# Seven-product matmul phases of a decoder trunk: sums of the moving operand on another engine, a second place for shared sums, stores two steps later, differences spread

## The chip, the cores and the metric

The kernel runs on one core of a Trainium2 chip. The metric is the device time in microseconds (us). Three runs of the kernel before gave 1637.1 (median), 1635.87 and 1639.43.

## What is computed

One layer of a hybrid decoder trunk over 1056 tokens: 1024 of a prompt and 32 new ones (8 sequences of 4). A normalised input goes through one wide projection; sliding-window attention and a gated linear recurrence run side by side, their outputs are mixed by sigmoid gates, and an MLP and a per-layer embedding follow. The last part of the reference is the part that the change touches:

```python
rnn = (h.astype(x.dtype) * jax.nn.gelu(gr)) @ lw['w_o_rnn']
mix = (jax.nn.sigmoid(ga_logit) * (att @ lw['w_o_attn']) + jax.nn.sigmoid(gr_logit) * rnn) @ lw['w_out']
x = x + mix
hmid = jax.nn.relu(rmsnorm(x, lw['norm2_g']) @ lw['w_up'])
x = x + (hmid * hmid) @ lw['w_down']
gate = jax.nn.sigmoid(rmsnorm(x, lw['ple_norm_g']) @ lw['w_ple_gate'])
x = x + gate * (p.astype(x.dtype) @ lw['w_ple'])
```

`D_MODEL` is 1024 and `D_FF` 4096. All data is float32.

## The kernel before

**Phases.** The matmuls from `w_o_rnn` to `w_down` run as ten phases of equal size (list `phases`): `rnn` (w_o_rnn), `out` (w_out), and then four times `up` and `down`, each on a quarter of the MLP's inner width. Each phase multiplies a 1024x1024 weight by a 1024x1056 moving operand. It cuts both into 2x2 blocks and computes seven products of blocks instead of eight, which needs sums of blocks on both sides and sums of the results (`PRODUCTS`: which weight sum meets which operand sum, q = 0 to 6). Blocks of the weight are called A11 to A22 and their sums S1 to S4; blocks of the operand B11 to B22 and their sums T1 to T4.

**Steps.** A product is four steps (p = 0 to 3, one for each 128 output rows); a step is 24 matmuls of 128x264, since each float32 operand is split into a high and a low part and three of the four part products are computed (lines 1432 to 1434). So a phase has 28 steps, and all phases 280. The main loop over `s` writes out the order of each engine by hand, step by step: `prepare` (the weights' high part by ScalarE, `w_high`, L1131, and low part by VectorE, `w_low`, L1136), `down_sums` (sums of weight blocks, by accumulating DMAs on GpSimd's queue, in every phase but the three later `up`), the step's matmuls, `evacuate` of the step before, the `hooks` of this step, and `prepare_b`. `flow.later(n, f)` runs f at the end of the n-th step from now, this one counted as the first. Each engine, and each DMA queue, works in the order in which its instructions were written out; a wait holds up all that stands behind it on the same engine or queue.

**The moving operand.** `prepare_b` does two things for the products to come. `b_sums` makes the operand's sums in place: for q = 2 with VectorE (L1150, L1151); for q = 3 and 4, in the phases rnn, out and the first up, with ScalarE (a negation, L1153) and accumulating DMAs from GpSimd's queue (L1154, L1156); in the phase down with VectorE, for q = 4 and 5 (L1158, L1160). `b_split` then splits a block into high (ScalarE, L1174) and low part (VectorE, L1175) in one of four places of `ring`; two places belong to one product, and a place is written again two products, eight steps, later. The half k2 = 0 of a product's sums is written out at the last step of the product two before it, its split at the first step of the product before it; the half k2 = 1 follows at the first and second step of the product before it. In the first up phase the split parts also go to DRAM (`xc_dram`, L1178, on the sync engine's queue), and the three later up phases read them from there (L1169) instead of splitting again.

**Evacuation.** `evacuate` adds a step's result to the quarters of the output to which it belongs (`put`, VectorE, L1227), or copies it where the quarter is empty (ScalarE, L1233). In phase out the quarters are the residual X, and products 1 to 3 are also gathered in a tile `shared`, one for each p (L1254 and L1227), which GpSimd's queue adds to other rows of X by accumulating DMAs (L1259): once after product 2, twice after product 3. Rows that are complete are squared and summed (`squares`, L1197, L1198) and scaled for the next phase (`scaled_row`, L1364). `mean_square` multiplies the sums of squares by a matrix of ones (L1352). In phase rnn, `mix` multiplies by a gate (L1336) and adds the attention part, twelve times of sixteen by an accumulating DMA (L1340).

**Hooks.** `hook(s, f)` puts f at step s. `differences(p)` (L1280), two subtractions on VectorE on rows of X that phase down adds to, stands at steps 84 to 87, the first four of the first down phase.

Of the kernel before, what the change touches and what calls it, by code (L numbers as in the profile page):

```python
# [13 lines left out]
F32 = mybir.dt.float32  # L14
F32R = mybir.dt.float32r
AF = mybir.ActivationFunctionType
ALU = mybir.AluOpType

P = 128
# [8 lines left out]
TH, CQ = T // 2, T // 4  # L28
# [62 lines left out]
def trunk(ctx: ExitStack, tc: tile.TileContext, I, O):  # L91
    nc = tc.nc
    PE, ACT, DVE, POOL, SP = nc.tensor, nc.scalar, nc.vector, nc.gpsimd, nc.sync

    def f32(ap):
        return ap.bitcast(F32)

    ctx.enter_context(tc.manual_schedule())
    flow = Flow()
# [856 lines left out]
    HALF = [slice(0, TH), slice(TH, T)]  # L956
# [95 lines left out]
    xc_dram = spill.tile([28, P, 2, TH], F32, name="xc_dram")  # L1052
    X, xn, shared = [None] * KT, [[None, None] for _ in range(4)], {}
# [14 lines left out]
    def b_view(ph_, k2, kh_, th_):  # L1068

        kind, f = phases[ph_]  # L1070
        if kind == "rnn":
            return [rnn[4 * kh_ + 2 * k2 + i][:, HALF[th_]] for i in range(2)]
        return [(xn if kind == "up" else hid)[k2 + 2 * kh_][th_]]
# [3 lines left out]
    def later_up(ph_):  # L1077
        kind, f = phases[ph_]
        return kind == "up" and f > 0
# [58 lines left out]
    def of_product(g):  # L1138
        return g // 7, g % 7

    def b_sums(g, k2):

        ph_, q = of_product(g)
        kind, f = phases[ph_]
        if kind == "up" and f:
            return
        by_dma = kind != "down"
        for b11, b12, b21, b22 in zip(*(b_view(ph_, k2, kh_, th_) for kh_, th_ in ((0, 0), (0, 1), (1, 0), (1, 1)))):
            if q == 2:
                DVE.tensor_tensor(b12, b22, b12, op=ALU.subtract)  # L1150
                DVE.tensor_tensor(b11, b12, b11, op=ALU.add)  # L1151
            elif q == 3 and by_dma:
                ACT.activation(b11, b11, AF.Identity, scale=-1.0)  # L1153
                POOL.dma_start(b21, b11, accum_op=ALU.add)  # L1154
            elif q == 4 and by_dma:
                POOL.dma_start(b11, b22, accum_op=ALU.add)  # L1156
            elif q == 4:
                DVE.tensor_tensor(b21, b21, b11, op=ALU.subtract)  # L1158
            elif q == 5 and not by_dma:
                DVE.tensor_tensor(b11, b22, b11, op=ALU.subtract)  # L1160

    def b_split(g, k2):
        ph_, q = of_product(g)
        kind, f = phases[ph_]
        r = ring[2 * (g % 2) + k2]
        u = 4 * q + 2 * k2
        if kind == "up" and f:
            for k in range(2):
                SP.dma_start(f32(r[:, k]), xc_dram[u + k])  # L1169
            return  # L1170
        src = b_view(ph_, k2, *B_HOME[PRODUCTS[q][1]])
        for i, x in enumerate(src):
            hi, lo = (r[:, :, n, :] if len(src) == 1 else r[:, i, n, :] for n in range(2))
            ACT.copy(hi, x)  # L1174
            DVE.tensor_tensor(lo, x, f32(hi), op=ALU.subtract)  # L1175
        if kind == "up":
            for k in range(2):
                SP.dma_start(xc_dram[u + k], f32(r[:, k]))  # L1178

    x2 = {}  # L1180

# [11 lines left out]
    def squares(j, th_, eng):  # L1193
        x, o = X[j][:, HALF[th_]], HALF[th_]
        if th_ in summed:
            s = chunk_tmp("t")
            ACT.activation(s, x, AF.Square)  # L1197
            eng.tensor_tensor(ssq2[:, o], ssq2[:, o], s, op=ALU.add)  # L1198
        else:
            ACT.activation(ssq2[:, o], x, AF.Square)  # L1200
            summed.add(th_)
# [11 lines left out]
    def third_gain(j, th_):  # L1213
        third_high(j, th_)
        third_low(j, th_)

    def evacuate(u, ps):
        ph_, q, p = u // 28, u % 28 // 4, u % 4
        kind, f = phases[ph_]

        def quarter(m, th_):
            r = p + 4 * m
            t = hid[r // 2][th_][:, r % 2] if kind in ("up", "rnn") else X[r][:, HALF[th_]]
            return t.rearrange("p (c n) -> p c n", c=2)

        q11, q12, q21, q22 = (quarter(m, th_) for m in range(2) for th_ in range(2))
        put = lambda to, of, op: DVE.tensor_tensor(to, of, ps, op=op)  # L1227
        if kind in ("rnn", "up"):

            sign = 1.0 if later_up(ph_) else -1.0  # L1230
            add, neg = ALU.add, ALU.add if later_up(ph_) else ALU.subtract
            if q < 2:
                ACT.activation((q11, q12)[q], ps, AF.Identity, scale=sign)  # L1233
            for to, of, op in ([], [(q11, q11, neg)], [(q12, q12, add)], [(q22, q12, neg)], [(q21, q22, add)],
                               [(q22, q22, add), (q12, q12, add)], [(q12, q12, neg)])[q]:
                put(to, of, op)
            if q not in (1, 4, 5, 6):
                return
            th_ = int(q > 4)
            if kind == "rnn":  # L1240
                mix(p + 4 * (q in (4, 5)), th_)
                return
            h, r = (q12, q11, q21, q22)[(6, 1, 4, 5).index(q)], ssq[:, HALF[th_]].rearrange("p (c n) -> p c n", c=2)

            def squared_relu():
                DVE.scalar_tensor_tensor(h, h, 0.0, r, op0=ALU.max, op1=ALU.mult)  # L1246
                ACT.activation(h, h, AF.Square, scale=0.5)  # L1247
            flow.later(1, squared_relu)
            return
        if kind == "out":  # L1250

            if q == 1:
                shared[p] = big.tile([P, TH], F32, tag=f"d{4 + p}", name="shared")
                ACT.activation(shared[p].rearrange("p (c n) -> p c n", c=2), ps, AF.Identity, scale=-1.0)  # L1254
            sh = shared[p].rearrange("p (c n) -> p c n", c=2) if q else None
            for to, op in ([(q11, 0)], [(q11, 0)], [(sh, 1)], [(sh, 0)], [(q21, 1)], [(q22, 1), (q12, 1)], [(q12, 0)])[q]:
                put(to, to, (ALU.subtract, ALU.add)[op])
            for r, th_ in {2: ((p, 1),), 3: ((p + 4, 0), (p + 4, 1))}.get(q, ()):
                POOL.dma_start(X[r][:, HALF[th_]], shared[p], accum_op=ALU.add)  # L1259
            if q in (1, 4, 5, 6):  # L1260
                j, th_ = p + 4 * (q in (4, 5)), int(q > 4)
                flow.later(1, lambda: (squares(j, th_, DVE), scaled_row(j, th_)))
            return

        last = ph_ == NPH - 1
        for to, op in ([(q11, ALU.subtract)], [(q11, ALU.subtract), (q22, ALU.subtract)], [(q22, ALU.add)],
                       [(q22, ALU.subtract), (q12, ALU.add)], [(q21, ALU.add)],
                       [(q22, ALU.add)] + ([] if last else [(q21, ALU.subtract)]), [(q12, ALU.subtract)])[q]:
            put(to, to, op)
        if last:  # L1270
            if q == 1:
                flow.later(8, lambda: third_gain(p, 0))
            elif q == 4:
                DVE.tensor_tensor(q21, q21, q22, op=ALU.add)
                flow.later(5, lambda: third_gain(p + 4, 0))
# [50 lines left out]
    def load_sigma(j, th_, place):  # L1326
        sigma_of[j, th_] = place
        SP.dma_start(place, s_dram[j, :, HALF[th_]])
# [4 lines left out]
    def mix(j, th_):  # L1333
        th_ = int(th_)
        u, a = hid[j // 2][th_][:, j % 2], A[j][:, HALF[th_]]
        DVE.tensor_tensor(u, u, sigma_of[j, th_], op=ALU.mult)  # L1336
        if j < 4 and th_ == 1:
            DVE.tensor_tensor(u, u, a, op=ALU.add)
        else:
            POOL.dma_start(u, a, accum_op=ALU.add)  # L1340
# [30 lines left out]
    def hook(s, fn, *args):  # L1371
        hooks.setdefault(s, []).append(lambda: fn(*args))


    for j in range(4):
        hook(2 + j, sigmoid, j, 0)
        hook(10 + j, load_sigma, j + 4, 0, rnn[j][:, HALF[1]])
        hook(12 + j, lambda j=j: load_sigma(j + 4, 1, sigmas[j]))
        hook(14 + j, sigmoid, j + 4, 0)
        hook(15 + j, load_sigma, j, 1, rnn[j + 4][:, HALF[0]])  # L1380
        hook(18 + j, sigmoid, j + 4, 1)
        hook(21 + j, load_residual, j)
        hook(22 + j, sigmoid, j, 1)
        hook(26 + j, load_residual, j + 4)
        hook(84 + j, differences, j)
    hook(28 + 23, second_norm, 0)
    hook(28 + 30, summed.clear)
    hook(56 + 2, second_norm, 1)
# [30 lines left out]
    for s in range(STEPS):  # L1419
        ph_, q, p = s // 28, s % 28 // 4, s % 4  # L1420
# [7 lines left out]
        for c in range(2):  # L1428
            ps = a[:, c, :CQ]
            for k in range(4):  # L1430
                r = ring[2 * (s // 4 % 2) + k // 2][:, k % 2, :, c * CQ:(c + 1) * CQ]
# [79 lines left out]
    for th_ in range(2):  # L1511
        for j in range(KT):
# [8 lines left out]
            for c in range(2):  # L1521
                oc = slice(c * CQ, (c + 1) * CQ)
                ps = a[:, c, :CQ]
# [63 lines left out]
```

## Time and profile before

| | us |
|---|---|
| median of 3 runs | 1637.1 |
| the profiled execution | 1636.45 |
| its span, first to last instruction | 1634.7 |
| phase rnn, from 649.2 | 91.9 |
| phase out, from 741.1 | 100.9 |
| first phase up, from 842.0 | 96.8 |
| first phase down, from 938.8 | 89.7 |
| second phase up, from 1028.5 | 82.1 |
| second phase down, from 1110.6 | 82.2 |

All rows below are of one profiled execution. PE is TensorE, DVE VectorE, ACT ScalarE, POOL GpSimd, SP the sync engine. Times run from the start of the span. A phase is found in the trace by its matmuls: the first 24 of lines 1432 to 1434 are step 0, the next 24 step 1, and so on; it begins where its first matmul begins. PEclk is the clock that TensorE was granted, as a share of 2.4 GHz. The DMA share is the mean busy share of the 16 DMA engines by their packets, and can exceed 1 since packets overlap.

### The profile page before, as it was taken

Reading aid. Unit: us, or ns where it says so; the run is one execution under the profiler, and the core shown is the slowest. Engines: PE = TensorE matmul, PEld = TensorE weight load, DVE = VectorE, ACT = ScalarE, POOL = GpSimd, SP = SyncE. Lnnn points to the kernel's source line nnn. Section 1 sums busy time; section 2 is a strip of 40 time slices with the busy share of each in tenths; the row PEclk is TensorE's granted clock in tenths of the full one; section 3 lists DMA queues with packets and bytes.
Section 4 is the critical chain, followed back from the end, with each engine's and each line's share of the span. In section 5 each row is a group of like instructions: output and inputs, shape, how many; then the busy total and the mean of one; then the engine's idle time right before and its main releaser. Section 6 shows DMA issues by size and latency. Waiting matters only on the chain.

```text
span 1634.7 us, 28211 instructions
## 1 busy us (share of the span) xinstructions
PE 1561.1 (95%) x11488; PEld 1537.9 (94%) x11488; DVE 1072.1 (66%) x1481; ACT 838.7 (51%) x1324; POOL 329.6 (20%) x327
## 2 busy tenths in 40 slices
PE   5989999999999999989989989999999999999997
PEld 5989999999999999989888889999999999999997
DVE  6797665444334353667677698579857985799862
ACT  6555666777667756553484433344334433446341
POOL 4552225232222311322312010001000100012010
PEclk9999999999999999999999999999999999999999
DMA  5522112133321176799979964486348634880332
GB/s 177 81 78 69 54 68 80 59 119 109 109 96 59 46 254 197 162 256 228 209 220 245 307 119 146 177 299 116 134 180 302 115 132 185 298 171 9 97 86 75
DMA packets 186138, 242.08 MB, mean 148 GB/s; under 512 B 22004, under 2 KB 134820, under 8 KB 185992
## 3 DMA queue, kind: packets, MB, share of 16 engines
q1 hardware_dynamic: 150680, 197.93, 36.5%
q0 software_dynamic: 35328, 42.34, 15.7%
q8 instruction: 91, 1.49, 0.4%
q14 instruction: 39, 0.32, 0.1%
HBM read 160.32 MB, written 38.60 MB: 122 GB/s over the span
## 4 chain that ended last, share of the span: by engine, by line
PE 72%; DVE 10%; DMA 8%; ACT 5%; issue 3%; POOL 1%; SPq 1%; ACTq 0%; POOLq 0%; DVEq 0%
PE acc L1433 12%; PE acc L1432 12%; PE acc L1434 12%; PE m L225 9%; PE m L227 9%; PE m L226 9%; DMA gl<-gl 2%; PE acc L1527 2%; PE acc L1529 2%; PE acc L1528 2%; DMA xn<-xn 2%; DMA X<-shared 2%; DVE wul L1136 1%; DVE ring L1175 1%; DMA wblock<-in_w_out 1%
## 5 line engine op out<-in xcount | busy, mean ns | idle before, releaser
L1432 PE MATMUL acc<-ring,wuh 128*128 128x264 f32 x2240 | 641.8, 287 | 24.8 <-DVE hid L1227 12.0
L1433 PE MATMUL acc<-ring,wuh 128*128 128x264 f32 x2240 | 643.6, 287 | 2.5 <-DVE ring L1175 2.5
L1434 PE MATMUL acc<-ring,wul 128*128 128x264 f32 x2240 | 643.9, 287 | 0.0
L1432 PEld LDWEIGHTS acc<-ring,wuh 128*128 128x128 f32 x2240 | 427.2, 191 | 29.1 <-ACT ring L1174 9.5
L1433 PEld LDWEIGHTS acc<-ring,wuh 128*128 128x128 f32 x2240 | 425.5, 190 | 5.0 <-DVE ring L1175 5.0
L1434 PEld LDWEIGHTS acc<-ring,wul 128*128 128x128 f32 x2240 | 425.3, 190 | 0.0
L225 PE MATMUL m<-xa,wh 128*128 128x352 f32 x912 | 298.9, 328 | 0.1
L226 PE MATMUL m<-xb,wh 128*128 128x352 f32 x912 | 295.0, 323 | 1.3 <-DVE xb L319 1.2
L227 PE MATMUL m<-xa,wl 128*128 128x352 f32 x912 | 295.4, 324 | 0.0
L1131 ACT CAST wuh<-wblock 128x1024 fp32r<-128x1024 f32 x100 | 104.5, 1048 | 193.5 <-PE acc L1433 158.1
L226 PEld LDWEIGHTS m<-xb,wh 128*128 128x128 f32 x912 | 173.4, 190 | 2.4 <-DVE xb L319 2.1
L225 PEld LDWEIGHTS m<-xa,wh 128*128 128x128 f32 x912 | 172.9, 190 | 1.1 <-ACT xa L318 0.4
L227 PEld LDWEIGHTS m<-xa,wl 128*128 128x128 f32 x912 | 172.9, 190 | 0.0
L1227 DVE TENSOR_TENSOR X<-X,acc 128x528 f32<-128x528 f32 x180 | 121.1, 697 | 32.4 <-PE acc L1434 28.0
L1227 DVE TENSOR_TENSOR hid<-hid,acc 128x528 f32<-128x528 f32 x140 | 96.2, 700 | 59.5 <-PE acc L1434 37.1
L1136 DVE TENSOR_TENSOR wul<-wblock,wuh 128x1024 fp32r<-128x1024 f32 x100 | 122.0, 1220 | 18.8 <-ACT wuh L1131 18.8
L1096 POOL DMA_DIRECT2D wblock<-wblock x14 | 18.6, 1536 | 492.4 <-DMA wblock<-in_w_down 375.1
L1175 DVE TENSOR_TENSOR ring<-hid,ring 128x1056 fp32r<-128x1056 f32 x70 | 88.8, 1268 | 30.4 <-ACT ring L1174 30.4
L1174 ACT CAST ring<-hid 128x1056 fp32r<-128x1056 f32 x70 | 74.0, 1070 | 59.0 <-DVE hid L1151 15.1
L1247 ACT ACTIVATE hid<-hid 128x528 f32<-128x528 f32 x64 | 41.3, 645 | 92.0 <-DVE hid L1246 92.0
L154 DVE TENSOR_TENSOR wl<-wraw,wh 128x1024 fp32r<-128x1024 f32 (+1 forms) x45 | 54.7, 1216 | 48.7 <-ACT wh L153 48.5
L857 DVE SCALAR_TENSOR_TENSOR rt<-a,rt 128x1056 f32<-128x1056 f32 x8 | 10.1, 1258 | 109.3 <-ACT rt L854 109.3
(348 smaller groups left out, 2525.3 us busy)
## 6 DMA issues: line engine op xcount, KB each, us to landing
ring<-xc_dram SPq DMA_DIRECT2D x84, 528.0 KB
wblock<-in_w_down SPq DMA_DIRECT2D x40, 512.0 KB
wraw<-in_w_in SPq DMA_DIRECT2D x34, 512.0 KB
wblock<-in_w_up SPq DMA_DIRECT2D x34, 512.0 KB
xc_dram<-ring SPq DMA_DIRECT2D x28, 528.0 KB
wblock<-wblock POOLq DMA_DIRECT2D x28, 512.0 KB, 7.4
s<-wblock POOLq DMA_DIRECT2D x28, 512.0 KB, 5.7
wblock<-in_w_o_rnn SPq DMA_DIRECT2D x10, 512.0 KB
```

What stands on the lines that cost most here:

```text
L154: low.tensor_tensor(lo[:, :nk, :], raw[:, :nk, :], f32(hi[:, :nk, :]), op=ALU.subtract)
L225: PE.matmul(ps, wh, xh, start=k == 0, stop=False)
L226: PE.matmul(ps, wh, xl, start=False, stop=False)
L227: PE.matmul(ps, wl, xh, start=False, stop=k == nk - 1)
L1131: ACT.copy(units[u][0], w_view(ph_, PRODUCTS[q][0], p2))
L1136: DVE.tensor_tensor(lo, w_view(ph_, PRODUCTS[q][0], p2), f32(hi), op=ALU.subtract)
L1174: ACT.copy(hi, x)
L1175: DVE.tensor_tensor(lo, x, f32(hi), op=ALU.subtract)
L1227: put = lambda to, of, op: DVE.tensor_tensor(to, of, ps, op=op)
L1432: PE.matmul(ps, wh[:, k, m], r[:, 0, :], start=k == 0, stop=False)
L1433: PE.matmul(ps, wh[:, k, m], r[:, 1, :], start=False, stop=False)
L1434: PE.matmul(ps, wl[:, k, m], r[:, 0, :], start=False, stop=k == 3)
```

## The change

In phases rnn, out and the first up, `b_sums` makes the sums for q = 4 and 5 by VectorE, as in phase down; the negation and the accumulating DMAs of these sums are gone. The tile `shared` has two places: the sum after product 3 is written to the second one, from the first, and each DMA reads the place of its product. The stores of the split parts to `xc_dram` are written out two steps later (by `flow.later`). The four `differences` stand at steps 70, 75, 80 and 85 (56 + 14, 19, 24, 29) instead of 84 to 87; steps 56 to 83 are the first up phase.

```diff
--- before.py
+++ after.py
@@ -1144,19 +1144,13 @@
         kind, f = phases[ph_]
         if kind == "up" and f:
             return
-        by_dma = kind != "down"
         for b11, b12, b21, b22 in zip(*(b_view(ph_, k2, kh_, th_) for kh_, th_ in ((0, 0), (0, 1), (1, 0), (1, 1)))):
             if q == 2:
                 DVE.tensor_tensor(b12, b22, b12, op=ALU.subtract)
                 DVE.tensor_tensor(b11, b12, b11, op=ALU.add)
-            elif q == 3 and by_dma:
-                ACT.activation(b11, b11, AF.Identity, scale=-1.0)
-                POOL.dma_start(b21, b11, accum_op=ALU.add)
-            elif q == 4 and by_dma:
-                POOL.dma_start(b11, b22, accum_op=ALU.add)
             elif q == 4:
                 DVE.tensor_tensor(b21, b21, b11, op=ALU.subtract)
-            elif q == 5 and not by_dma:
+            elif q == 5:
                 DVE.tensor_tensor(b11, b22, b11, op=ALU.subtract)
 
     def b_split(g, k2):
@@ -1174,8 +1168,7 @@
             ACT.copy(hi, x)
             DVE.tensor_tensor(lo, x, f32(hi), op=ALU.subtract)
         if kind == "up":
-            for k in range(2):
-                SP.dma_start(xc_dram[u + k], f32(r[:, k]))
+            flow.later(2, lambda: [SP.dma_start(xc_dram[u + k], f32(r[:, k])) for k in range(2)])
 
     x2 = {}
 
@@ -1250,13 +1243,14 @@
         if kind == "out":
 
             if q == 1:
-                shared[p] = big.tile([P, TH], F32, tag=f"d{4 + p}", name="shared")
-                ACT.activation(shared[p].rearrange("p (c n) -> p c n", c=2), ps, AF.Identity, scale=-1.0)
-            sh = shared[p].rearrange("p (c n) -> p c n", c=2) if q else None
-            for to, op in ([(q11, 0)], [(q11, 0)], [(sh, 1)], [(sh, 0)], [(q21, 1)], [(q22, 1), (q12, 1)], [(q12, 0)])[q]:
-                put(to, to, (ALU.subtract, ALU.add)[op])
+                shared[p] = big.tile([P, 2, TH], F32, tag=f"d{4 + p}", name="shared")
+                ACT.activation(shared[p][:, 0].rearrange("p (c n) -> p c n", c=2), ps, AF.Identity, scale=-1.0)
+            sh, sh2 = (shared[p][:, i].rearrange("p (c n) -> p c n", c=2) for i in range(2)) if q else (None, None)
+            for to, of, op in ([(q11, q11, 0)], [(q11, q11, 0)], [(sh, sh, 1)], [(sh2, sh, 0)], [(q21, q21, 1)],
+                               [(q22, q22, 1), (q12, q12, 1)], [(q12, q12, 0)])[q]:
+                put(to, of, (ALU.subtract, ALU.add)[op])
             for r, th_ in {2: ((p, 1),), 3: ((p + 4, 0), (p + 4, 1))}.get(q, ()):
-                POOL.dma_start(X[r][:, HALF[th_]], shared[p], accum_op=ALU.add)
+                POOL.dma_start(X[r][:, HALF[th_]], shared[p][:, q - 2], accum_op=ALU.add)
             if q in (1, 4, 5, 6):
                 j, th_ = p + 4 * (q in (4, 5)), int(q > 4)
                 flow.later(1, lambda: (squares(j, th_, DVE), scaled_row(j, th_)))
@@ -1382,7 +1376,7 @@
         hook(21 + j, load_residual, j)
         hook(22 + j, sigmoid, j, 1)
         hook(26 + j, load_residual, j + 4)
-        hook(84 + j, differences, j)
+        hook(56 + (14, 19, 24, 29)[j], differences, j)
     hook(28 + 23, second_norm, 0)
     hook(28 + 30, summed.clear)
     hook(56 + 2, second_norm, 1)
```

## Rows read from the trace of the kernel before

**Rows 1.** The page's busy table: busy us (share of the span), instructions.

```profile
PE 1561.1 (95%) x11488; PEld 1537.9 (94%) x11488; DVE 1072.1 (66%) x1481; ACT 838.7 (51%) x1324; POOL 329.6 (20%) x327
```

**Rows 2.** Phases: start:end, length, PE, PEld, DVE, ACT, POOL busy, PEclk, DMA share.

```profile
649.20:741.10 91.90, 85.36 (x672) 84.62 (x673) 64.85 (x88) 46.61 (x69) 27.82 (x28) 0.96 0.92 215
741.10:842.00 100.90, 89.54 (x678) 87.00 (x677) 71.14 (x85) 53.28 (x67) 24.32 (x24) 0.95 0.91 203
842.00:938.80 96.80, 88.71 (x679) 86.24 (x677) 67.46 (x80) 51.18 (x64) 13.90 (x12) 0.96 0.95 280
938.80:1028.50 89.70, 84.96 (x673) 83.97 (x674) 78.35 (x92) 29.81 (x31) 7.69 (x6) 0.98 0.53 128
1028.50:1110.60 82.10, 82.10 (x674) 82.10 (x673) 54.83 (x65) 33.47 (x42) 5.15 (x4) 1.00 0.74 243
1110.60:1192.80 82.20, 82.20 (x675) 82.20 (x674) 68.25 (x78) 27.81 (x28) 5.15 (x4) 1.00 0.46 122
```

**Rows 3.** The same view, ten stretches of whole steps.

```profile
696.24:720.62 24.38, 17.89 (x123) 17.11 (x121) 11.95 (x16) 11.06 (x17) 2.57 (x3) 0.86 0.95 237
758.74:772.89 14.15, 10.39 (x74) 10.18 (x73) 7.53 (x8) 7.22 (x10) 2.56 (x2) 0.88 0.98 190
778.75:786.25 7.50, 6.35 (x50) 5.97 (x49) 7.12 (x8) 7.02 (x9) 5.25 (x5) 1.00 0.74 122
795.05:816.14 21.09, 18.84 (x147) 17.87 (x145) 12.22 (x14) 6.76 (x9) 6.91 (x8) 1.00 1.09 239
819.16:833.22 14.06, 9.85 (x54) 8.89 (x53) 10.43 (x14) 12.20 (x17) 2.60 (x2) 0.76 0.42 129
847.89:855.55 7.66, 6.98 (x55) 6.66 (x53) 5.33 (x6) 7.63 (x10) 1.45 (x2) 1.00 1.17 265
864.33:886.98 22.65, 19.16 (x146) 17.91 (x145) 17.90 (x21) 13.81 (x17) 7.86 (x7) 1.00 1.02 270
904.58:920.02 15.44, 12.17 (x74) 11.68 (x73) 9.37 (x11) 7.28 (x9) 0.00 (x0) 0.78 1.03 385
925.89:942.04 16.15, 15.50 (x123) 14.90 (x121) 14.45 (x19) 9.89 (x13) 2.60 (x2) 1.00 0.97 260
947.90:975.68 27.78, 23.05 (x170) 22.27 (x169) 27.18 (x33) 9.50 (x10) 5.12 (x4) 0.94 0.66 123
```

**Rows 4.** Waits, 649 to 1028 us: who <- whom: us in total, times, longest.

```profile
DVE ring L1175 <- ACT ring L1174: 55.4, 23, 10.2
...
ACT ring L1174 <- DMA gl<-gl: 22.0, 8, 8.5
...
ACT wuh L1131 <- DMA s<-wblock: 12.8, 1, 12.8
...
ACT ring L1174 <- DMA xn<-xn: 11.8, 2, 8.9
...
ACT ring L1174 <- DMA hid<-hid: 9.4, 3, 5.2
...
DVE shared L1227 <- DMA X<-shared: 9.0, 4, 4.9
...
ACT ring L1174 <- DVE xn L1151: 7.2, 2, 3.9
```

**Rows 5.** DMA issues: queue, operation, count, KB each, median us to landing.

```profile
X<-shared POOLq DMA_DIRECT2D x12, 264.0 KB, 14.0
...
gl<-gl POOLq DMA_DIRECT2D x8, 264.0 KB, 18.6
```

**Rows 6.** VectorE's groups, 649 to 1028 us: xcount | busy us, mean ns.

```profile
L1280 DVE TENSOR_TENSOR X<-X 128x528 f32<-128x528 f32 x8 | 5.3, 699 | 0.0
...
L1151 DVE TENSOR_TENSOR gl<-gl 128x528 f32<-128x528 f32 x4 | 2.8, 708 | 0.1
...
L1151 DVE TENSOR_TENSOR xn<-xn 128x1056 f32<-128x1056 f32 x2 | 2.5, 1258 | 0.1
```

**Rows 7.** The view of rows 2, 720 to 765 us.

```profile
720.00:765.00 45.00, 44.77 (x365) 44.55 (x364) 39.11 (x51) 20.49 (x26) 10.45 (x11) 1.00 1.09 278
```

## The prediction

> **What bounds the kernel now.** I read the busy shares first, then the time of each phase, then the stretches that are longer than their work, and last who waits in them. TensorE is busy for 95% of the span [rows 1], which looks as if nothing were left. The table by phase corrects that [rows 2]: every phase has the same matmuls (28 steps of 24, so 672; the count is a few higher or lower), and the fifth and the sixth take 82.1 and 82.2 us, 2.93 us for a step, with the clock at 1.00. The first four take 91.9, 100.9, 96.8 and 89.7 us, 379.3 together where four quiet ones take 328.6. So 50.7 us are lost there, and this is all that can be won: the change touches no line that runs ahead of 649 us or after 1028 us.
>
> Where they are lost is seen in ten stretches that begin and end with a step [rows 3]. Length less steps x 2.93 us gives: a (696 to 721, 5 steps) 9.7; b (759 to 773, 3) 5.4; c (779 to 786, 2) 1.6; d (795 to 816, 6) 3.5; e (819 to 833, 2) 8.2; f (848 to 856, 2) 1.8; g (864 to 887, 6) 5.1; h (905 to 920, 3) 6.6; i (926 to 942, 5) 1.5; k (948 to 976, 7) 7.3. That is 50.7 us, all of it. In a, b, e, h and k the granted clock is 0.76 to 0.94: behind a gap TensorE comes back at the lower of its two levels (1.2 GHz) for a few us, so a gap that goes takes this with it.
>
> Who waits [rows 4]: ScalarE's copy of the moving operand's high part (L1174) waits 22.0 us for the sums of gl, 11.8 for those of xn and 9.4 for those of hid, all DMAs; VectorE's low part waits behind it. VectorE itself waits 9.0 us for DMAs that read the shared sums. ScalarE waits 12.8 us, once, for a weight sum by DMA. These DMAs are slow because they stand in one queue: half of gl's take over 18.6 us from issue to landing, half of the shared ones over 14.0 [rows 5], while a product of four steps lasts 11.7.
>
> **The change part by part.**
>
> *The operand's sums.* In the phases rnn, out and up, 16 accumulating DMAs go (8 of 264 KB, 8 of 528 KB) with 8 negations on ScalarE, which I count at nothing. VectorE gets 8 subtractions of 128x528 in rnn, 8 x 0.708 = 5.7 us, and 4 of 128x1056 in out and in up, 4 x 1.258 = 5.0 us each; the same operations run today for T2 and T3 [rows 6]. The new order is that of the phase down, a sum just ahead of the split that reads it. Stretches a and h are this wait and nothing else: in a ScalarE waits for gl, in h for xn. What hides the new work is VectorE's idle time: 64.85 us busy of 91.9 in rnn and 71.14 of 100.9 in out would become 70.6 and 76.1, where down runs 68.25 of 82.2 without a lost step [rows 2]. If that cover went, it would cost its 5 us in a phase. I leave 0.5 us of a (ends 0 and 1) and 0.5 of h (0 and 3). In up two of the sums, 2.5 us, fall into the end of g, where the sums for T2 and T3 already make ScalarE wait 7.2 us for VectorE [rows 4], which stays. Its bounds are 2.5 us more and, as two negations leave the same steps, 2.5 us less; I take 0.8 more, since the row that is nearest is a VectorE that is 17.90 us busy of 22.65 [rows 3]. So g keeps 5.9 (2.6 to 7.6).
>
> *The second place for the shared sums.* The later sum no longer overwrites what a DMA still reads, so the 9.0 us of VectorE's wait go, and the four 528 KB sums of hid no longer stand between these DMAs. Late next are the X rows themselves: the products that add to X four steps after the issue, 11.7 us, need the DMA landed, and it takes 14.0 today behind the traffic that leaves. I take d as gone (0 to 3.5). Stretch e begins where VectorE and ScalarE come out of d with work piled up, and holds the matmuls with ones for the second norm, as f does; f has no other cause and loses 1.8 us, so 1.8 stays in each. I leave 0.8 more in e (ends 1.8 and 5).
>
> *Stretches b and c.* They follow the weight sum that ScalarE waits 12.8 us for. No edit touches it. From 720 to 765 us the DMA engines are full (share 1.09 [rows 7]). The bytes stay; what moves is the start. The load of the block behind it waits on VectorE's last weight split of the phase, and that stood behind the ring wait of stretch a. Without a, the loads start earlier against the steps, at most by the 9.7 us of a. I take 0.5 left in b and in c; the ends are nothing and all of it (5.4 and 1.6).
>
> *The stores two steps later.* On the sync queue a store waits for VectorE's low part and holds up the weight loads queued behind it; now those pass ahead. No wait of TensorE in [rows 4] ends on such a load, so I count no gain. The bound to the worse is a rival below, since the ring's places are written again eight steps after a split.
>
> *The differences.* Eight of 0.699 us [rows 6], 5.6 us, stand today at the first four steps of the phase down, and run in the stretch k and just ahead of it. There VectorE is busy 27.18 us of 27.78 [rows 3]: VectorE sets the pace in k, and what is taken away is won. Three pairs of the four, 4.2 us, go to earlier steps, so k keeps 7.3 - 4.2 = 3.1 (ends 0, and 8 if VectorE arrives late from the phase up). The 4.2 us land in up, whose VectorE goes from 67.46 to 67.46 + 5.0 + 4.2 = 76.7 us, 93% of a quiet phase. So i stays at 1.5 (0 to 4).
>
> By the Trainium skill, Perfetto Trace Analysis, Optimizing Scalar/DVE Operations, a saturated VectorE should hand work to ScalarE or GpSimd; this change does the reverse in the phase next to k. The row of k, 98% busy, bears the rule out for that stretch; by the rule the sum would be that of the first rival.
>
> *The sum.* Left: a 0.5, b 0.5, c 0.5, d 0, e 2.6, f 1.8, g 5.9, h 0.5, i 1.5, k 3.1, together 16.9. Saved: 50.7 - 16.9 = 33.8 us. The profiled execution took 1636.45 us, its span 1634.7; 1636.45 - 33.8 = 1602.6. The median of the runs is 0.65 us above that execution, so 1603.
>
> **The rivals.** *VectorE becomes the bound.* Over up and the first down it is busy 67.46 + 78.35 = 145.8 us of 186.5 [rows 2], 78%; the rest is waiting, 55.4 us in all four phases for ScalarE's high part [rows 4]. If it does no better, its 150.8 us take 192.8, a loss of 28.5 where I have 1.8 + 5.9 + 0.5 + 1.5 + 3.1 = 12.8: 1603 + 15.7 = 1619. For it speaks k; against it, that much of the 55.4 us is the wait for DMAs that go, and that a quiet down phase reaches 83%. *The full DMA stretch stays*: b and c are bound by bytes, and keep 7.0 in place of 1.0: 1609. For it speaks the share of 1.09, against it the late start. *The later stores hold up the ring, slower than before*: a store leaves six steps, 17.6 us, until its place is written. If it lands L us after its issue, each of the seven splits that follow waits L - 17.6. That outweighs 33.8 us, and 0.2% with it, from L = 22.9 us; at 25 us it gives 7 x 7.4 = 52 us and 1655. The slowest landing in the rows is 18.6, in a queue full of accumulations [rows 5], which would cost 7 us. *The change doesn't do what it says*: the splits wait as long for VectorE as for the DMAs, and the time stays at 1637.
>
> **How the numbers follow.** Forecast 0.66; VectorE the bound 0.12; full DMA stretch 0.15; slower by the stores 0.04; nothing 0.03. The likeliest gives 1603. The range is 1593 to 1619: the low end is every open stretch at its lower bound (e 1.8, f 1.8, g 2.6, i 1.5 left, 7.7 in all, so 43 us saved and 1594, rounded outward), the high end the first rival, with the second inside. 0.2%, 3.3 us, is about what a measurement of this kernel can tell from no change. Faster by more: 0.66 + 0.12 + 0.15 = 0.93; within: 0.03; slower: 0.04.
>
> **What would show it.** Right: no wait of L1174 for gl, hid or xn sums; none of VectorE for a DMA of shared; rnn at some 83 us, out at 86, up at 92 and down at 85; the clock near 1.00 in rnn. The first rival shows as up and down at 94 us and more with VectorE over 90% busy and its waits for L1174 unbroken; the second as a wait of ScalarE for a weight sum at the product S2 of the phase out; the slower one as L1174 waiting for the DMA from ring to xc_dram. The prediction is wrong if out stays over 95 us although no operand sum is a DMA, or if a phase after 1028 us leaves 82 us.

## The result, and the profile after

The changed kernel takes 1609.26 us (median of 4 runs, 1607.53 to 1609.85), the kernel before on the same chip 1637.69: a ratio of 0.9825, 95% interval 0.9808 to 0.9842. It is 28.4 us faster, where 34 were forecast. The profiled execution took 1609.85 us, its span 1607.7. Lines have moved: the ring's high and low part are L1168 and L1169 now, the sums of T4 and T1 L1152 and L1154 (new on VectorE), the squared relu L1239 and L1240, the sums out of PSUM L1220, the copy out of PSUM L1226, the DMAs into X L1253; L1090 to L1136 are as they were.

The busy line of the page, which answers to [rows 1]:

```profile
PE 1552.7 (97%) x11488; PEld 1531.2 (95%) x11488; DVE 1084.9 (67%) x1497; ACT 832.7 (52%) x1316; POOL 315.2 (20%) x311
```

GpSimd issues 16 DMAs fewer, VectorE does 16 instructions more. The six phases, as in [rows 2] (start:end, length, PE, PEld, DVE, ACT and POOL busy, granted clock, DMA share, GB/s):

```profile
651.00:733.00 82.00, 82.00 (x673) 82.00 (x674) 70.25 (x98) 44.49 (x65) 20.87 (x20) 1.00 0.89 217
733.00:823.80 90.80, 86.09 (x679) 84.49 (x677) 73.36 (x86) 50.34 (x63) 23.24 (x22) 0.98 0.93 203
823.80:916.70 92.90, 85.64 (x677) 83.31 (x677) 76.78 (x91) 50.42 (x63) 7.84 (x7) 1.00 0.83 264
916.70:1002.40 85.70, 83.40 (x672) 82.41 (x673) 74.56 (x86) 29.73 (x31) 7.69 (x6) 1.00 0.55 133
1002.40:1084.50 82.10, 82.10 (x674) 82.10 (x673) 54.78 (x65) 33.45 (x42) 5.14 (x4) 1.00 0.75 245
1084.50:1166.70 82.20, 82.20 (x675) 82.20 (x674) 68.30 (x78) 27.81 (x28) 5.12 (x4) 1.00 0.45 120
```

The four phases take 351.4 us in place of 379.3: 27.9 us are gone and 22.8 of the 50.7 lost ones are left. rnn has no loss any more, at a clock of 1.00 where it was 0.96. Ahead of rnn the new execution is 1.8 us later (651.0 against 649.2) in work that no edit touches; over the executions shown below, the start of rnn lies anywhere from 649.6 to 652.6. The same view for the stretches that are still longer than their steps:

```profile
753.50:763.90 10.40, 7.66 (x51) 7.45 (x50) 7.78 (x8) 5.68 (x9) 3.92 (x3) 0.84 0.90 172
769.70:776.70 7.00, 6.37 (x51) 5.98 (x50) 7.00 (x8) 4.04 (x5) 1.74 (x2) 1.00 0.34 57
806.00:814.10 8.10, 7.20 (x55) 6.57 (x53) 7.96 (x11) 6.28 (x9) 1.40 (x2) 1.00 0.24 70
817.10:827.10 10.00, 9.55 (x75) 8.99 (x74) 9.19 (x13) 7.43 (x11) 2.56 (x2) 1.00 1.14 242
829.90:838.40 8.50, 6.95 (x54) 6.64 (x53) 6.12 (x7) 8.47 (x12) 0.00 (x0) 1.00 0.75 282
847.30:869.90 22.60, 19.12 (x147) 17.87 (x146) 17.85 (x21) 10.86 (x14) 3.39 (x3) 1.00 0.94 251
899.10:907.10 8.00, 6.42 (x51) 6.03 (x50) 7.70 (x10) 3.47 (x5) 0.00 (x0) 1.00 0.52 212
912.90:920.00 7.10, 6.45 (x51) 6.05 (x50) 6.77 (x9) 3.25 (x5) 0.03 (x1) 1.00 1.15 234
925.80:946.70 20.90, 18.60 (x147) 17.82 (x146) 20.30 (x23) 9.51 (x10) 3.84 (x3) 1.00 0.70 136
```

These are 2, 2, 2, 3, 2, 6, 2, 2 and 6 steps of 2.93 us, so they lose 4.5 (b), 1.1 (c), 2.2 and 1.2 (e with its end), 2.6 (f), 5.0 (g), 2.1 (new, steps 79 and 80), 1.2 (i) and 3.3 us (k). Stretches a, d and h are gone. Against the forecast of what would be left, b is 4.0 us over, steps 79 and 80 2.1, e and f together 1.6, c 0.6; a, g and h are 1.9 below.

The waits of 651 to 1028 us, against [rows 4]:

```profile
ACT hid L1240 <- DVE hid L1239: 30.7, 17, 3.2
DVE ring L1169 <- ACT ring L1168: 29.2, 19, 5.3
...
ACT ring L1168 <- DVE hid L1150: 12.6, 3, 5.5
...
ACT wuh L1131 <- DMA s<-wblock: 11.7, 1, 11.7
...
ACT ring L1168 <- DVE hid L1152: 9.7, 4, 4.3
...
ACT ring L1168 <- DVE xn L1150: 7.2, 2, 3.9
ACT ring L1168 <- DVE hid L1154: 6.9, 4, 2.5
```

No operand sum is a DMA, so ScalarE's 43.2 us of waits for the DMAs of gl, xn and hid are gone, and VectorE's 9.0 us for the shared sums too; VectorE's wait for the high part fell from 55.4 to 29.2 us. In place of the 43.2 us ScalarE waits 21.3 us for the sums that are new on VectorE: 2.4 in rnn, 10.7 in out and 8.2 in up. The 12.8 us for the weight sum of S2 became 11.7: this is stretch b.

### The profile page after: what moved, and what is told of

The parts are those of the page before. It is cut to its first block, busy times and chain, and to the rows that moved or that the text cites. A ratio compares the mean times of both kernels' runs of the same rounds, so it can differ in the third digit from the quotient of the medians.

```text
span 1607.7 us, 28168 instructions
## 1 busy us (share of the span) xinstructions
PE 1552.7 (97%) x11488; PEld 1531.2 (95%) x11488; DVE 1084.9 (67%) x1497; ACT 832.7 (52%) x1316; POOL 315.2 (20%) x311
## 4 chain that ended last, share of the span: by engine, by line
PE 75%; DVE 11%; ACT 6%; DMA 4%; issue 3%; SPq 0%; ACTq 0%; DVEq 0%; POOLq 0%
PE acc L1427 13%; PE acc L1426 13%; PE acc L1428 13%; PE m L225 9%; PE m L227 9%; PE m L226 9%; PE acc L1521 2%; PE acc L1523 2%; PE acc L1522 2%; DVE wul L1136 2%; DMA s<-in_w_out 1%; DMA wraw<-in_w_in 1%; DVE ring L1169 1%; PE m L641 1%; ACT ring L1168 1%
## 5 line engine op out<-in xcount | busy, mean ns | idle before, releaser
L1426 PEld LDWEIGHTS acc<-ring,wuh 128*128 128x128 f32 x2240 | 422.7, 189 | 15.5 <-ACT ring L1168 4.8
L1427 PEld LDWEIGHTS acc<-ring,wuh 128*128 128x128 f32 x2240 | 421.3, 188 | 3.0 <-DVE ring L1169 2.9
L1220 DVE TENSOR_TENSOR X<-X,acc 128x528 f32<-128x528 f32 x180 | 121.2, 698 | 27.7 <-PE acc L1428 24.7
L1220 DVE TENSOR_TENSOR hid<-hid,acc 128x528 f32<-128x528 f32 x140 | 96.4, 700 | 57.4 <-PE acc L1428 34.9
L1136 DVE TENSOR_TENSOR wul<-wblock,wuh 128x1024 fp32r<-128x1024 f32 x100 | 122.0, 1220 | 18.8 <-ACT wuh L1131 18.8
L1096 POOL DMA_DIRECT2D wblock<-wblock x14 | 18.6, 1562 | 499.6 <-DMA wblock<-in_w_down 374.2
L1169 DVE TENSOR_TENSOR ring<-hid,ring 128x1056 fp32r<-128x1056 f32 x70 | 88.8, 1269 | 30.7 <-ACT ring L1168 30.7
L1168 ACT CAST ring<-hid 128x1056 fp32r<-128x1056 f32 x70 | 74.1, 1070 | 58.6 <-DVE hid L1154 18.4
L1240 ACT ACTIVATE hid<-hid 128x528 f32<-128x528 f32 x64 | 41.3, 645 | 95.5 <-DVE hid L1239 95.5
```

Of the source, the lines that this page charges most:

```text
L1136: DVE.tensor_tensor(lo, w_view(ph_, PRODUCTS[q][0], p2), f32(hi), op=ALU.subtract)
L1426: PE.matmul(ps, wh[:, k, m], r[:, 0, :], start=k == 0, stop=False)
L1427: PE.matmul(ps, wh[:, k, m], r[:, 1, :], start=False, stop=False)
```

## The experiments

Each stretch in the texts below is named as in the prediction. The columns b to k of the table are what a stretch loses: its length less its steps x 2.93 us, from the starts of the steps' first matmuls. There b is steps 35 to 37, e 51 to 56, f 57 to 62, g 63 to 72, "79" 79 to 82 and k 86 to 94.

| kernel | median us | rnn | out | up | down | b | e | f | g | 79 | k |
|---|---|---|---|---|---|---|---|---|---|---|---|
| before | 1637.7 | 91.9 | 100.9 | 96.8 | 89.7 | 5.4 | 8.2 | 1.8 | 5.1 | 0.3 | 7.3 |
| changed | 1609.3 | 82.0 | 90.8 | 92.9 | 85.7 | 4.5 | 3.4 | 2.7 | 5.0 | 2.1 | 3.3 |
| e1 sums only | 1611.1 | 82.0 | 90.9 | 90.6 | 89.2 | 4.4 | 3.4 | 2.6 | 5.0 | 0.0 | 6.8 |
| e2 one place | 1608.6 | 82.0 | 90.2 | 92.9 | 85.7 | 4.1 | 3.4 | 2.6 | 5.0 | 2.0 | 3.3 |
| e3 stores at once | 1609.6 | 82.2 | 90.0 | 93.0 | 85.7 | 4.1 | 3.4 | 2.6 | 5.0 | 2.0 | 3.3 |
| e4 differences in down | 1610.7 | 82.2 | 90.1 | 90.5 | 89.6 | 4.0 | 3.5 | 2.7 | 5.0 | 0.0 | 7.2 |
| e5 later X rows | 1606.9 | 82.2 | 86.1 | 92.9 | 85.7 | 0.0 | 3.4 | 2.7 | 5.0 | 2.0 | 3.3 |
| e6 split first | 1611.0 | 82.1 | 94.7 | 91.0 | 85.8 | 5.3 | 6.3 | 2.6 | 5.0 | 0.2 | 3.3 |
| e7 norm later | 1608.7 | 82.0 | 90.4 | 92.4 | 85.2 | 4.4 | 3.4 | 0.2 | 4.6 | 5.2 | 3.1 |
| e8 GpSimd | 1616.5 | 82.0 | 90.1 | 101.5 | 84.5 | 4.1 | 3.4 | 2.7 | 16.0 | 0.0 | 2.1 |
| e9 = e5 + relu apart | 1595.9 | 82.2 | 86.1 | 87.0 | 82.2 | 0.0 | 3.4 | 2.7 | 1.9 | 0.0 | 0.0 |
| e10 = e9 + norm later | 1595.4 | 82.2 | 86.0 | 84.1 | 83.2 | 0.0 | 3.4 | 0.2 | 1.2 | 0.0 | 0.8 |
| e11 = e9 + first norm later | 1597.8 | 82.2 | 87.4 | 88.0 | 82.1 | 0.7 | 2.6 | 3.9 | 1.9 | 0.0 | 0.0 |
| e12 = e9 + differences in down | 1599.5 | 82.2 | 87.8 | 87.1 | 83.3 | 0.7 | 3.4 | 2.7 | 1.9 | 0.0 | 1.2 |

The runs of one kernel scatter by 1 to 5 us. Phases that two kernels share agree to 0.2 us, but for out, which moves by up to 1.8 us, in b, in c and between the two (e11 and e12 have no edit ahead of step 51 that e9 lacks). So the parts are judged by the phases, and less than 2 us in out is not read as an effect.

**The parts of the change, alone and undone.** e1 is the kernel before with the operand's sums of the change and nothing else:

```diff
-        by_dma = kind != "down"
 ...
-            elif q == 3 and by_dma:
-                ACT.activation(b11, b11, AF.Identity, scale=-1.0)
-                POOL.dma_start(b21, b11, accum_op=ALU.add)
-            elif q == 4 and by_dma:
-                POOL.dma_start(b11, b22, accum_op=ALU.add)
             elif q == 4:
                 DVE.tensor_tensor(b21, b21, b11, op=ALU.subtract)
-            elif q == 5 and not by_dma:
+            elif q == 5:
```

> The kernel before with one part of the change alone: the moving operand's sums on VectorE. If the working of the prediction holds, stretches a and h go (9.7 and 6.6 us, less the 1.0 left), rnn takes 82 to 83 us, VectorE still waits for the shared sums (d and e stay within 3 us of before) and the differences still stand in down (k keeps its 7.3 or more): 16 to 24 us less than before, 1613 to 1621. The rival, VectorE as the bound, has the added 15.7 us of subtractions come back as stalls in out, up and down: less than 10 us gained, over 1627.

It takes 1611.1 us, a ratio of 0.9835 (0.9818 to 0.9851): the whole change has 0.9825. By the phases it is worth 26.6 of the 27.9 us. Its phases (columns as above):

```profile
651.80:733.80 82.00, 81.99 (x672) 82.00 (x673) 70.24 (x98) 44.48 (x65) 20.88 (x20) 1.00 0.89 216
733.80:824.70 90.90, 85.90 (x679) 84.35 (x677) 73.32 (x86) 50.22 (x63) 20.78 (x20) 0.98 0.88 195
824.70:915.30 90.60, 85.29 (x677) 83.35 (x677) 73.20 (x85) 50.49 (x63) 10.34 (x8) 1.00 0.91 280
915.30:1004.50 89.20, 84.46 (x673) 83.66 (x674) 78.25 (x92) 29.83 (x31) 7.69 (x6) 0.98 0.53 128
```

It gained more than expected, because d, and e but for 3.4 us, went with it: VectorE waits for no shared sum, though there is still one place. The DMAs into X land sooner: hid's four large sums, of which before two were issued ahead of these DMAs and two between them, are gone from the queue. Median landing in the phase out, first of e1, then of e2:

```profile
X<-shared POOLq DMA_DIRECT2D x12, 264.0 KB, 7.5
```

```profile
X<-shared POOLq DMA_DIRECT2D x12, 264.0 KB, 7.1
```

It was 14.0 us [rows 5], and the place is written again four steps, 11.7 us, later. e2 is the changed kernel with

```diff
-shared[p] = big.tile([P, 2, TH], F32, tag=f"d{4 + p}", name="shared")
+shared[p] = big.tile([P, TH], F32, tag=f"d{4 + p}", name="shared")
```

and the sums of both products in that one tile.

> The changed kernel with one place for the shared sums again. If the second place is what took VectorE's 9.0 us of waits for the shared sums, the waits come back and with them d (3.5 us) and up to 3 us of e: 3 to 9 us slower than the changed kernel. The rival: the DMAs into X now land in 7.4 us (median), before the place is written again four steps (11.7 us) later, because hid's sums no longer stand in their queue; then the second place is worth under 1 us.

VectorE has no wait for these DMAs in e2 either, and out takes 90.2 us against 90.8. The second place is worth nothing here: the rival named ahead of the run came. (Whether it would have helped with the operand's sums still on DMAs wasn't tried.) e3 issues the stores at once:

```diff
-flow.later(2, lambda: [SP.dma_start(xc_dram[u + k], f32(r[:, k])) for k in range(2)])
+for k in range(2):
+    SP.dma_start(xc_dram[u + k], f32(r[:, k]))
```

> The changed kernel with the stores of the split operand issued at once. The prediction put this part at nothing: within 1.5 us of the changed kernel, up at 92 to 94 us. A rival: a store that waits for VectorE's low part held up the weight loads behind it on the sync queue; then up or the first down phase is over 2 us longer.

Up takes 93.0 and down 85.7 us: nothing, as the prediction had it. e4 puts the differences back into down:

```diff
-hook(56 + (14, 19, 24, 29)[j], differences, j)
+hook(84 + j, differences, j)
```

> The changed kernel with the differences of X at the first four steps of the phase down again. By the prediction down gets 4.2 us longer (85.7 to some 90) and up stays, so some 4 us slower. The rival: VectorE is as full in up, and the stalls that are new there at steps 79, 80, 83 and 84 (3.2 us) are the price of the differences; then up gets 3 us shorter, down 4 us longer, and the time moves by 1 us or so.

Phases up and down of e4:

```profile
824.50:915.00 90.50, 85.22 (x676) 83.25 (x676) 73.10 (x85) 50.46 (x63) 7.98 (x7) 1.00 0.86 271
915.00:1004.60 89.60, 84.81 (x672) 83.84 (x673) 78.42 (x92) 29.82 (x31) 7.69 (x6) 0.98 0.53 128
```

Down is 3.9 us longer and up 2.4 shorter than in the changed kernel, so spreading the differences brings 1.5 us net. The stalls at steps 79 and 80 are their price: without the differences there, these two steps lose 0.0. How they cause it is seen on ScalarE in the changed kernel (start us, us; in brackets the idle time before, and for whom):

```profile
894.92 0.65 ACT L1240 ACTIVATE hid<-hid 128x528 f32<-128x528 f32 x1 [3.22 <-DVE hid L1239]
895.47 1.03 ACT L1131 CAST wuh<-s 128x1024 fp32r<-128x1024 f32 x1
896.41 2.00 ACT L1090 ACTIVATE wblock<-wblock 128x1024 f32<-128x1024 f32 x2
898.32 1.06 ACT L1168 CAST ring<-xn 128x1056 fp32r<-128x1056 f32 x1
```

A pair of differences (1.4 us) stands on VectorE ahead of the relu's first half, so ScalarE's square (L1240) starts late; behind it a weight copy and two negations are queued, and only then the ring's high part, for which VectorE and then TensorE wait.

**Stretch b.** e5 writes out the loads of X rows 4 to 7 seven steps later (`load_residual` takes the tile as before and hands its `SP.dma_start` to `flow.later`):

```diff
-hook(26 + j, load_residual, j + 4)
+hook(26 + j, load_residual, j + 4, 7)
```

> The changed kernel with the loads of X rows 4 to 7 (2.1 MB) issued seven steps later, so that they no longer run beside the load of S2 and its weight sum. If stretch b is bound by the bytes ahead of and beside the weight sum, that sum lands 4 us and more earlier, ScalarE's 11.7 us wait for it shrinks to under 8, and b falls from 4.5 to under 1.5 us: 3 to 4 us faster than the changed kernel. The rival: the chain is S2's own load behind the blocks A21 and A22 and X rows 0 to 3, so that what is queued after it does not matter: b stays at 3.5 to 4.5.

b is 0.0 and out takes 86.1 us, what was forecast for it. By the medians the gain is 2.4 us only (1606.9 against 1609.3): the profiled execution, 1603.95 us, is e5's fastest by 2.8. But b is 0.0 to 0.7 in all five profiled executions with this edit (e5, e9 to e12), and 4.0 to 5.3 in the eight of the changed kernel and the others without it. The weight sum of S2 (L1102), 700 to 770 us, in the changed kernel and then in e5:

```profile
L1102 POOL DMA_DIRECT2D s<-wblock x2: 1279/1286/1294, 738.6 to 743.6; - x2
...
  DMA s<-in_w_out: 13.5, 2
...
  ACT wuh L1131: 11.7, 1
...
DMA to landing us min/median/max: 12.5/12.8/13.0
```

```profile
L1102 POOL DMA_DIRECT2D s<-wblock x2: 1279/1288/1297, 735.8 to 740.5; - x2
...
  DMA wblock<-wblock: 11.5, 2
...
  ACT wuh L1131: 6.7, 1
...
DMA to landing us min/median/max: 9.5/9.7/9.8
```

The phase out began at 731.9 us in e5 and at 733.0 in the changed kernel. Against that, the first sum is issued 1.7 us sooner, no longer held by the load of S2 but by the block's own sum, takes 3.2 us less to land, and so lands 4.9 us sooner; ScalarE waits 5.0 us less. Only the X loads have moved (in the traces three of the four: they leave at 744 to 745 us in place of 733 to 738, the first at 728.6 in place of 729.7), so b was bound by what runs beside its transfers.

**Stretches g, 79 and k.** e6 issues the weight work of a step behind the operand's split:

```diff
         prepare(s)
-        down_sums(s)
 ...
         prepare_b(s)
+        down_sums(s)
```

> The changed kernel with the weight work of down_sums (ScalarE's negations and the weight DMAs) issued behind the operand's split of the same step. At steps 49 and 78 two negations of 1.05 us stand on ScalarE ahead of the split, and VectorE waits 3.1 and 3.9 us for it. If that is what makes steps 51 and 79 long, the stall at 79 (2.0 us with 80) goes below 0.7 and step 51 loses up to 1 us: 1.5 to 3 us faster. The rival: the stall at 79 is VectorE's own load with the differences; it stays over 1.5.

The stall at 79 fell to 0.2 us, so the two negations were needed for it; but e rose from 3.4 to 6.3, and the time from 1609.3 to 1611.0 (b's 5.3 is within what out moves by). One order that helps at step 78 harms at 50, where ScalarE's squares for the norm come behind the negations. What of the 2.9 us in e is from these squares and what from later weight DMAs wasn't taken apart.

> The changed kernel with the second norm of the second half ten steps later (step 68 in place of 58); its result is first read at step 77. If stretch g is VectorE working off what the norm put in front of it at steps 58 to 60 (some 2.8 us of work and 1.9 us of waiting for ScalarE), g falls from 5.0 to 1.5 us or less and f from 2.7 to 0, while the matmuls with ones (1.6 to 1.9 us) are paid at step 68: 3 to 5 us faster. The rival, on which the prediction rested: g is the sums of the operand and the splits themselves, and stays over 3.5.

e7 has `hook(56 + 12, second_norm, 1)` in place of `56 + 2`. f went (2.7 to 0.2), g only from 5.0 to 4.6, of which part is the ones matmuls in their new place, and the loss at 79 rose from 2.1 to 5.2: up takes 92.4 us, 0.5 less. The time won was given back at the next place where VectorE and ScalarE were late. So the norm isn't g's only cause, and up as a whole was held by something else.

e8 has the differences on GpSimd, at steps 68 to 71 (`POOL.tensor_tensor(x, x, x22, ...)`).

> The changed kernel with the differences of X on GpSimd, at steps 68 to 71. If VectorE's load is what down and up lack, up returns to 90.6 us (as without the differences) and down stays at 85.7: 2.3 us faster. The rival: GpSimd's subtractions slow VectorE's beside them (over 1.0 us for one of 128x528 that takes 0.70 alone), or come late, and up or down is longer than in the changed kernel.

The rival came, far larger. VectorE, and then GpSimd, in 856.6 to 873 us:

```profile
857.41 11.67 DVE L1239 SCALAR_TENSOR_TENSOR hid<-hid,ssq 128x528 f32<-128x528 f32 x1
871.24 0.70 DVE L1220 TENSOR_TENSOR hid<-hid,acc 128x528 f32<-128x528 f32 x1 [2.15 <-ACT hid L1226]
```

```profile
857.13 1.28 POOL L1111 DMA_DIRECT2D s<-wblock  x1 [5.86 <-ACT hid L1226]
857.90 10.60 POOL L1274 TENSOR_TENSOR X<-X 128x528 f32<-128x528 f32 x8
```

GpSimd's queue doesn't follow TensorE's steps: the rows of X were final, and all eight subtractions ran in one go as soon as the weight DMA ahead of them (L1111) was issued. A VectorE operation of 0.70 us took 11.67 beside them, g grew to 16.0 us, and up to 101.5. Steps 79 and 80 lost nothing.

e9 leaves the work alone and parts the relu's halves:

```diff
-            def squared_relu():
-                DVE.scalar_tensor_tensor(h, h, 0.0, r, op0=ALU.max, op1=ALU.mult)
-                ACT.activation(h, h, AF.Square, scale=0.5)
-            flow.later(1, squared_relu)
+            flow.later(1, lambda: DVE.scalar_tensor_tensor(h, h, 0.0, r, op0=ALU.max, op1=ALU.mult))
+            flow.later(2, lambda: ACT.activation(h, h, AF.Square, scale=0.5))
```

> The kernel with the later X rows, and the two halves of the squared relu apart: VectorE's at the end of the step as now, ScalarE's square one step later. In g each step goes ScalarE's copy out of PSUM, VectorE's sum, VectorE's half of the relu, ScalarE's square, and the next copy stands behind that square on ScalarE: some 3.3 us a round, and 20.2 us of ScalarE's waits in up are for VectorE's half. If that round trip makes g, g falls from 5.0 to under 2 and the stall at 79 from 2.0 to under 1, with b still 0: 3 to 5 us faster than with the later X rows alone. The rival, the rule of the prediction, is that VectorE's plain load makes g and 79: then both stay within 1 us of what they were.

It takes 1595.9 us, a ratio of 0.9740 to the kernel before (0.9725 to 0.9754): 11 us less than e5, 9.4 by the four phases, where 3 to 5 were expected. g lost 3.1 of its 5.0 us, as expected, and 79, i and k went entirely, of which i and k were not: up 87.0, down 82.2. ScalarE in g of the changed kernel:

```profile
854.97 0.60 ACT L1226 ACTIVATE hid<-acc 128x528 f32<-128x528 f32 x1
857.09 0.65 ACT L1240 ACTIVATE hid<-hid 128x528 f32<-128x528 f32 x1 [1.51 <-DVE hid L1239]
857.64 0.59 ACT L1226 ACTIVATE hid<-acc 128x528 f32<-128x528 f32 x1
859.75 0.65 ACT L1240 ACTIVATE hid<-hid 128x528 f32<-128x528 f32 x1 [1.51 <-DVE hid L1239]
```

The copy out of PSUM stands behind the square of the step before, the square waits for VectorE's half, that for VectorE's sum, and that for the copy: a round of 2.7 us, 3.6 with a weight copy in it (853.5 to 857.1), where a step has 2.93. Neither engine is full, both are late. Phases up and down of e9:

```profile
819.20:906.20 87.00, 84.05 (x676) 83.12 (x677) 78.62 (x94) 51.99 (x65) 7.81 (x7) 1.00 0.91 285
906.20:988.40 82.20, 82.20 (x675) 82.20 (x674) 72.16 (x83) 28.47 (x29) 7.68 (x6) 1.00 0.55 136
```

VectorE does 94 instructions in up and 83 in down, where the changed kernel has 91 and 86: three that had been carried over into down are done in time. e12 puts the differences back into down in this kernel, with the edit of e4.

> The kernel with the later X rows and the halves of the relu apart, with the differences of X at the first four steps of the phase down again. By the prediction VectorE sets the pace in k (98% busy there), so its 4.2 us of work come back one for one: k goes from 0.0 to 4.2 and more, down to 86 us and over, some 4 us slower. The rival: k was the backlog that VectorE and ScalarE brought along from up, which is gone, and the differences fit into VectorE's idle time in down: k under 1.5, within 1.5 us in all.

Steps 86 to 94, the stretch k, in e4 and then in e12, which have the same work there, and last in e9, which has three of the four pairs of differences in up:

```profile
921.25:954.87 33.62, 28.87 (x219) 28.09 (x218) 32.25 (x40) 12.82 (x14) 6.40 (x5) 0.95 0.69 124
```

```profile
913.62:941.23 27.61, 26.89 (x218) 26.51 (x217) 27.02 (x33) 9.38 (x10) 5.12 (x4) 1.00 0.76 139
```

```profile
912.11:938.51 26.40, 26.40 (x219) 26.40 (x217) 25.80 (x30) 9.46 (x10) 5.12 (x4) 1.00 0.78 144
```

VectorE does 40 instructions in e4's k and 33 in e12's. Of the seven, five stand at the start (a pair of differences, a relu half, a split and a sum, some 4 us): in e12 they are done ahead of the stretch. The other two are at the end of e4's longer stretch. Without this backlog k loses 1.2 us with the differences in it, not 7.2. VectorE is 98% busy in e12's k too, and in e9's, where nothing is lost: the busy share alone doesn't tell whether VectorE sets the pace. The whole kernel, though, takes 1599.5 us, 3.5 more than e9, and not within 1.5 as the rival had it. Of the 2.9 us between the two profiled executions' four phases, down has 1.2 and out 1.7, ahead of every step at which the kernels differ; why out is longer stays open.

> The kernel of the run before with, besides, the second half's norm at step 68 in place of 58. If the round trip is gone, step 68 takes the matmuls with ones for 1.3 to 1.8 us and nothing else: f 0, g at most 1.8 more, so 1 to 2.5 us faster in all. The rival: the stall at 79 comes back over 3 us as it did with this edit alone, and nothing is gained.

With e7's edit added to e9, f is 0.2 and up 84.1, and 0.8 us come back in k and 0.6 in i. The four phases take 335.5 us, 2.0 less than in e9; the medians, 1595.4 and 1595.9, can't be told apart. By its phases this is the fastest kernel of the study, at 0.9735 (0.9721 to 0.9750) of the kernel before.

> The kernel with the halves of the relu apart and the first half's norm three steps later (54 in place of 51). Stretch e (3.4 us at 51 to 56) holds its ones matmuls. If they cost their own 1.6 us and the rest is work that waits around them, e falls by up to 1.8; if the place does not matter, e stays within 0.5 of 3.4.

e11 (`hook(28 + 26, second_norm, 0)`) moved 0.8 us out of e and 1.2 into f: nothing was gained.

## Why the prediction was right, and where its steps were not

The time lies in the range, 6 us above the likeliest value. Of the forecast's 16.9 us left, 22.8 were found, and the 1.8 us ahead of rnn came on top.

*The operand's sums, a and h.* Right in mechanism, and mis-sized to the safe side: 0.5 us was left in each, none remained. The cover named for the added VectorE work held in rnn (70.25 us busy of 82.0) and in out.

*The second place, d and part of e.* The outcome was right and the cause wrong. d did go, but with the sums (e1), and the place itself is worth nothing (e2). The prediction had the right observation at hand, that four 528 KB sums stand between the DMAs into X, and the distance of 11.7 us, but used both only for the X rows behind and not for the place: the landing fell from 14.0 to 7.4 us, below 11.7, and so the wait was gone before the second place could help.

*Stretches b and c.* Here the forecast failed: 0.5 us was taken as left in each, 4.5 and 1.1 were, and the second rival, the full DMA stretch, describes b. The failed step is that without a the loads would start earlier against the steps by up to 9.7 us. When TensorE stood in a, the steps stood with it: the issue of the block's load (L978) lay 21.1 us ahead of the phase out before and lies 22.1 ahead after, so 1 us was won of up to 9.7. e5 shows that the transfers beside it decide; the sign that the prediction named for this rival, ScalarE's wait for the weight sum of S2, is there with 11.7 us. c stays at 0.8 to 1.4 us with b gone, within its bounds.

*e and f.* 1.6 us over the forecast: e 3.4, with its end at steps 54 to 56, for 2.6, and f 2.7 for 1.8. In f TensorE waits 1.5 us for the last sum of squares ahead of the ones matmuls; moved to step 68 it costs no such wait (e7, e10).

*The stores.* Right: nothing either way (e3).

*The differences, k, i and the first rival.* k was forecast at 3.1 and has 3.3, but the net of the move is 1.5 us, not 4.2, since up lost 2.4: that 4.2 us find room in up was wrong, as they stood ahead of a chain between two engines and not merely in a busy engine's idle time. Nor was k itself what it was taken for. That VectorE is 98% busy there is so, and its work is won one for one as long as it is late; but it was late because of up (e9, e12). The first rival, VectorE as the bound, falls with the same runs: in e9 it does 78.62 us of work in 87.0 of up, and all of k in time. g, 5.0 us for 5.9, was put down to VectorE's load and the splits; most of it, 3.1 us, was the round trip. So the 3.3 us in k that match the forecast's 3.1 are luck: the reason given for them was wrong.

The prediction gave the advice of the Trainium skill, Perfetto Trace Analysis, Optimizing Scalar/DVE Operations, as a "should"; the page says only that handing work on "may make sense", and that between VectorE and GpSimd it "might not help". Here it cost 7 us (e8), and k's 98% didn't bear the advice out, since e9 has 98% there without a loss.

*Two loose readings that decided nothing.* The 18.6 us called the slowest landing is a median; the slowest of these sums took 21.9 us. And the low end of the range took i at 1.5 us, though its own bound was 0.

## What to carry to other kernels

A saving that takes a stall of the bounding engine away need not start DMAs earlier against that engine's own steps, since the steps move too; ask which distance in steps has changed. Two engines that hand work back and forth inside a step, in order, can be late with neither of them full: try the second half a step later before moving work from one to the other. A stretch in which an engine is 98% busy may be working off what an earlier stretch left: count its instructions in both. And where several edits are meant for one wait, the first may empty it for all: here one of four edits brought 26.6 of 27.9 us.

## What the runs showed of the hardware

A VectorE operation with both inputs in SBUF, 0.70 us alone, took 11.67 us while GpSimd did eight subtractions back to back (10.60 us in all; e8), although its record begins 0.49 us ahead of GpSimd's first. By the Trainium skill, SBUF — State Buffer, SBUF: two separate sides, such an operation and a GpSimd instruction that reads SBUF exclude each other, and the one that starts first holds the ports for its whole instruction. The trace agrees with the exclusion; it doesn't agree that the first by the records wins, and the block lasted for the whole run of eight rather than one instruction. Which of the two had the ports first, the records don't show.
